# One level of Strassen's scheme for w_up, and w_down as a stage of its own, in a float32 two-block transformer step

## The chip, the cores and the metric

The kernel runs on one core of one Trainium2 chip. The metric is the device time of one execution in microseconds. PE is TensorE, DVE VectorE, ACT ScalarE, POOL GpSimd and SP SyncE, which issues the DMAs here.

## What is computed

Two transformer blocks on 1024 tokens of width 1024, in float32. The change lies in the last part of the second block, a feed-forward network with a short causal convolution over the tokens on one half of its hidden width, and the gate of a per-token embedding behind it. In outline, with h the normalized input:

```python
a, b = jnp.split(h @ w_up, 2, axis=-1)          # w_up: 1024 x 6144
hidden = gelu(conv3(a, ffn_conv_w, ffn_conv_b)) * b   # conv3: three taps, causal, per channel
x = x + rms_norm(hidden @ w_down, g_ffn_post)   # w_down: 3072 x 1024
gate = sigmoid(rms_norm(x, g_ple_gate) @ w_ple_gate)
out = x + gate * rms_norm(p @ w_ple_proj, g_ple_post)
```

## The kernel before, in words

**Precision.** Every float32 product is made of three matmuls of a rounded type (`mm3`, L229 to L235): both operands are split into a high part and the rest (`split`, L73 to L79: ACT rounds, DVE or POOL subtracts), and hi x hi, lo x hi and hi x lo are added up in one PSUM bank. A bank holds 128 x 512; there are eight, five of them under the name mm and three under tr.

**Weights.** A `Chunk` is a piece of a weight. `queue` puts chunks in a list, and `pump` fetches the next one as soon as a raw buffer is free (a DMA on SP, L183, tile wr) and splits it as soon as a pair of buffers wh and wl is free. The program is written with a clock of its own (`tick`, `later`), by which later steps of norm chains are put between the matmuls; the order on each engine comes from that and from a scheduler behind it, and on the chip each engine works through its own order.

**Up.** h is kept transposed in h3h and h3l (its high part and rest), k along partitions, 1024 tokens along the columns. The 3072 hidden channels come in 24 chunks of 128; each chunk c has two blocks of w_up (the one that is convolved, u, and the one that multiplies it). `dense_t_steps` takes a block and one half of the tokens (512 columns): eight k-tiles, 24 matmuls into one bank. The first four blocks take the first half of the tokens before the second, because the norm chains of the last tokens (`mix_add`, L2020: POOL adds to tile max, L2030 nxn, then transposes on PE, L328) still run. `ffn` (L2063) holds `emit`: for a u block ACT copies the bank to fu (L2080) and starts fg (L2081), DVE adds the two earlier taps (L2084, twice), ACT applies Gelu (L2087). For a b block DVE multiplies (L2090) and the result is split into fhh and fhl.

**Down.** `contract` takes two chunks of hidden, and for each of eight token tiles and two column halves it adds six matmuls in a bank and then, on DVE, the bank to the tile acc in SBUF (L2105). Eleven contracts lie between the up blocks, the last two behind them. Every tile of acc is complete only in the last one.

**Behind it.** `finish_pair` (L2275), for two token tiles at a time, is a chain of squares (ACT), rstd and norm (DVE, L2297), residual (POOL, L2298), squares, rstd and xn (DVE, L2306), and transposes (`to_hT`, L322). It feeds the product with w_ple_gate, 48 matmuls for each token tile (tiles fhT, flT), whose result og is multiplied and added (L2264, L2265) and stored.

Of the kernel before, what the change touches and what calls it, by code (L numbers as in the profile page):

```python
# [15 lines left out]
F32 = mybir.dt.float32  # L17
# [31 lines left out]
class Chunk:  # L49


    def __init__(self, pieces, shape):
        self.pieces, self.shape = pieces, shape
        self.raw = self.hl = self.pool = self.rpool = None
        self.half = 0


class Kernel:
# [127 lines left out]

    def split_w(self, c):
        for e in self.wpools:
            if e[2] < e[1] and (e[3] is None or id(c) in e[3]):
                e[2] += 1  # L190
                c.pool = e
                c.hl = [e[0].tile(c.shape, F32R, name=n, tag=n, bufs=e[1]) for n in ("wh", "wl")]
                self.lo_engs = self.lo_engs[1:] + self.lo_engs[:1]
                self.split(*c.hl, c.raw, self.lo_engs[0], self.hi_eng)
                c.raw = None
                c.rpool[2] -= 1
                return True
        return False

    def need(self, c):  # L200
        assert c.hl is not None, "weight buffers"
        return c.hl
# [1860 lines left out]
    def ffn(self, pools, pu, acc, up, down, before_last, last):  # L2063


        nc = self.nc
        NC, G = DFF // P, 2
        st = {}

        def emit(b, half, ps):  # L2070
            c, hs, o = b // 2, slice(half * 512, half * 512 + 512), half * 512
            if b % 2 == 0:
                if half == 0:
                    st[c] = (pu.tile([P, 2 + S], F32, name="fu", tag="fu", bufs=2),
                             pu.tile([P, S], F32, name="fg", tag="fg", bufs=2),
                             *(pools[c // G % 2 == 0].tile([P, S], F32R, name=n, tag=n, bufs=G)
                               for n in ("fhh", "fhl")))
                    nc.gpsimd.memset(st[c][0][:, :2], 0.0)  # L2078
                u, g = st[c][:2]
                nc.scalar.activation(u[:, 2 + o:2 + o + 512], ps, AF.Copy)  # L2080
                nc.scalar.activation(g[:, hs], ps, AF.Identity, scale=self.fc_w[:, 2 * NC + c:2 * NC + c + 1],  # L2081
                                     bias=self.fc_b[:, c:c + 1])
                for k in range(2):
                    nc.vector.scalar_tensor_tensor(g[:, hs], u[:, k + o:k + o + 512],  # L2084
                                                   self.fc_w[:, k * NC + c:k * NC + c + 1], g[:, hs],
                                                   op0=OP.mult, op1=OP.add)
                nc.scalar.activation(g[:, hs], g[:, hs], AF.Gelu_apprx_tanh)  # L2087
            else:
                _, g, hi, lo = st[c]
                nc.vector.tensor_tensor(g[:, hs], ps, g[:, hs], op=OP.mult)  # L2090
                self.split(hi[:, hs], lo[:, hs], g[:, hs])

        def contract(c0, tiles=range(NT)):
            ws = [self.need(down[c]) for c in range(c0, c0 + G)]
            for t in tiles:
                ts = slice(t * P, (t + 1) * P)
                for n in range(2):
                    cs = slice(n * 512, n * 512 + 512)
                    ps = self.mmt()
                    for i in range(G):  # L2100
                        hi, lo = st[c0 + i][2:]
                        self.mm3(ps, (hi[:, ts], lo[:, ts]), (ws[i][0][:, 0, cs], ws[i][1][:, 0, cs]),
                                 i == 0, i == G - 1)
                    if c0:
                        nc.vector.tensor_add(acc[:, t, cs], acc[:, t, cs], ps)  # L2105
                    else:
                        nc.scalar.activation(acc[:, t, cs], ps, AF.Copy)
                last(c0 + G == NC, t)
            if NT - 1 in tiles:
                for c in range(c0, c0 + G):  # L2110
                    self.free(down[c])
                    del st[c]

        for n, _ in enumerate(self.dense_t_steps(up, self.hT, emit, first=4)):
            c = (n + 1) // 4 - 1
            if (n + 1) % 4 == 0 and c % G == 0 and c >= G:
                contract(c - G, range(NT if c < NC - G else 4))
        before_last()
        for tiles in (range(4), range(4, NT)):
            if tiles[0]:  # L2120
                contract(NC - 2 * G, tiles)
            contract(NC - G, tiles)

    def block2(self, es):
# [66 lines left out]
        up, down = [], []  # L2191
        for c in range(DFF // P):
            up += [self.chunk_t(blk(wu, i * DFF + c * P), KT) for i in range(2)]
            down.append(Chunk([(lambda r: r[:, 0], wd[c * P:(c + 1) * P])], [P, 1, D]))
        with ExitStack() as es2:
            self.add_w(es2, "wow", 2, side="right", only=sum(ch_o, []))
            self.mix_add(self.pool(es2, "onp", side="right"), ch_o, mT, a["g_mix_post_2"][0], a["g_ffn_pre_2"][0], self.hT)
            for c in range(DFF // P):
                self.queue(up[2 * c:2 * c + 2])
                if c % 2 == 0 and c:  # L2200
                    self.queue(down[c - 2:c])
            self.queue(down[-2:])
            self.until(lambda: self.hcount == NT)
        es_m.close()

        acc = self.pool(es, "accp", side="right").tile([P, NT, D], F32, name="acc")
        es_f, es_u, es_x = (ExitStack() for _ in range(3))
        pools = [self.pool(es_f, n, side="right") for n in ("ffnp", "ffnq")]
        self.add_w(es_f, "ffx", 2, side="right", only=up[:-4] + down[:-2])
        self.add_w(es_u, "ffw", 1, 2, side="right", only=up + down[:-4])  # L2210
        ch_p, fin = [], {}

        def before_last():
            es_u.close()
            es_h.close()
            self.hcount = 0
            self.add_w(es_x, "plew", 4)
            fp = fin["pool"] = self.pool(es_x, "finp")
            fin["g"], fin["gp"], fin["ge"] = (self.row(fp, a[n][0], D, n[:8]) for n in
                                              ("g_ffn_post_2", "g_ple_gate_2", "g_ple_post_2"))  # L2220
            fin["r"] = fp.tile([P, NT], F32, name="pler")
            nc.vector.tensor_add(self.ple_ss[:, 0], self.ple_ss[:, 0], self.ple_ss[:, 1])
            self.rstd(fp, fin["r"], self.ple_ss[:, 0], D)
            ch_p.extend(self.chunks_n(a["w_ple_gate_2"][0][:, c * 512:c * 512 + 512], KT, 512) for c in range(2))

        def step(p, n):
            for _ in range(n):
                next(fin[p], None)

        def last(b, t):  # L2230
            if (b, t) == (1, 1):
                fin.update({p: self.finish_pair(fin, acc, 2 * p) for p in range(4)})
            for p, n in {(1, 1): [(0, 1)], (1, 3): [(0, 2), (1, 1)], (0, 5): [(0, 1)], (0, 7): [(1, 2), (0, 1)], (1, 5): [(1, 1)], (1, 7): [(1, 1)]}.get((b, t), ()) if fin else ():
                step(p, n)

        self.ffn(pools, self.pool(es_u, "ffnu", side="right"), acc, up, down, before_last, last)
        es_f.close()

        self.add_w(es_f, "plex", 2, side="right")
# [10 lines left out]
        with self.tc.manual_schedule(engines={mybir.EngineType.Activation}):  # L2250
            for t in range(2):
                emb(t)
            for t in range(NT):
                p = t // 2
                x, e = fin["x", t], embs.pop(0)
                for c in range(2):
                    cs = slice(c * 512, c * 512 + 512)
                    ps = self.mmt()
                    for k in range(KT):
                        wh, wl = self.need(ch_p[c][k // 2])  # L2260
# [161 lines left out]
```

## Time and profile before

| | |
|---|---|
| median of 3 runs | 3548.86 us (3547.29 to 3552.15) |
| the profiled execution | 3554.52 us, of it span 3552.8 us |
| mean granted TensorE clock | 0.957 |
| busy: PE, DVE, ACT, POOL | 3224.1, 2231.8, 1546.0, 946.5 us |
| feed-forward stage, first to last w_up matmul | 2592.1 to 3376 us |
| w_ple_gate | 3425 us to the end |

A busy share is an average over stages with different limits. The stage that is changed starts at 2592 us; what bounds it is read from its own stretches. A matmul's duration (some 395 ns) is its time through the pipeline; the distance from one to the next is what counts, and it is read from how many start in a stretch.

### The profile page before, as it was taken

The numbers are of one execution on the slowest core, as the hardware profiler recorded it, in microseconds if no ns is written. First come the engines' busy times: TensorE is split into PE (matmuls) and PEld (weight loads), VectorE is DVE, ScalarE is ACT, GpSimd is POOL, SyncE is SP. The second block draws the span as 40 slices with busy tenths as digits, with TensorE's granted clock in tenths as the row PEclk, the third lists the DMA queues.
The fourth block names the chain that finished last, engine by engine and source line by source line (L and its number), as shares of the span: only waits on it lengthen the run. The fifth ranks groups of instructions, "written<-read, shape, count | busy, mean of one in ns | idle before, by whom it ended". The sixth has DMA issues, their size and how long they took to land. (4 is left out here: it accounts for less than half of the span.)

```text
span 3552.8 us, 40896 instructions
## 1 busy us (share of the span) xinstructions
PE 3224.1 (91%) x14381; PEld 2577.9 (73%) x14381; DVE 2231.8 (63%) x3579; ACT 1546.0 (44%) x2354; POOL 946.5 (27%) x704
## 2 busy tenths in 40 slices
PE   7987799789898898998888999999989999999987
PEld 4865577567677677777666887888668888888866
DVE  6799954578656899999885644124563444444364
ACT  3553222578523666666565763211343222222232
POOL 2133223355104666666440220000110000000024
PEclk9998899799999899999899999999999999999998
DMA  5211376662545899999864214333431111111032
GB/s 191 66 46 56 121 225 190 149 175 62 163 156 188 311 319 318 315 326 323 275 204 150 69 60 147 101 119 98 143 119 48 48 48 48 48 48 48 18 130 83
DMA packets 351644, 510.66 MB, mean 144 GB/s; under 512 B 32140, under 2 KB 183072, under 8 KB 351436
## 3 DMA queue, kind: packets, MB, share of 16 engines
q1 hardware_dynamic: 330304, 465.78, 40.4%
q0 software_dynamic: 11440, 24.77, 2.6%
q10 hardware_dynamic: 9692, 17.48, 1.5%
q8 instruction: 114, 1.87, 0.2%
q14 instruction: 94, 0.77, 0.1%
HBM read 426.47 MB, written 76.20 MB: 141 GB/s over the span
## 5 line engine op out<-in xcount | busy, mean ns | idle before, releaser
L79 DVE TENSOR_TENSOR wl<-wr,wh 128x1024 fp32r<-128x1024 f32 (+1 forms) x441 | 752.5, 1729 | 428.7 <-ACT wh L76 427.9
L76 ACT ACTIVATE wh<-wr 128x1024 fp32r<-128x1024 f32 x564 | 587.5, 1053 | 749.8 <-PE mm L234 234.9
L79 POOL TENSOR_TENSOR wl<-wr,wh 128x1024 fp32r<-128x1024 f32 x145 | 386.0, 2704 | 91.9 <-ACT wh L76 85.9
L235 PE MATMUL mm<-h3h,wl 128*128 128x512 f32 x768 | 303.8, 396 | 5.5 <-DVE wl L79 3.1
L234 PE MATMUL mm<-h3l,wh 128*128 128x512 f32 x768 | 303.4, 395 | 0.2 <-DVE h3l L79 0.2
L233 PE MATMUL mm<-h3h,wh 128*128 128x512 f32 x768 | 303.5, 395 | 0.0
L233 PE MATMUL mm<-h2h,wh 128*128 128x512 f32 x576 | 229.5, 399 | 1.2 <-ACT h2h L76 1.2
L235 PE MATMUL mm<-h2h,wl 128*128 128x512 f32 x576 | 227.4, 395 | 0.0
L234 PE MATMUL mm<-h2l,wh 128*128 128x512 f32 x576 | 227.3, 395 | 0.0
L2078 POOL MEMSET fu<- 128x2 f32 x24 | 2.3, 100 | 687.4 <-DVE fg L2084 682.7
L233 PE MATMUL mm<-wh,hTh 128*128 128x512 f32 (+1 forms) x368 | 145.6, 396 | 40.2 <-POOL wh L78 17.6
L235 PEld LDWEIGHTS mm<-h3h,wl 128*128 128x128 f32 x768 | 144.5, 188 | 41.1 <-DVE wl L79 4.4
L2105 DVE TENSOR_TENSOR acc<-acc,mm 128x512 f32<-128x512 f32 x176 | 119.0, 685 | 87.8 <-PE mm L235 87.7
L233 PEld LDWEIGHTS mm<-h3h,wh 128*128 128x128 f32 x768 | 144.5, 188 | 34.6 <-ACT wh L76 0.5
L234 PEld LDWEIGHTS mm<-h3l,wh 128*128 128x128 f32 x768 | 144.5, 188 | 34.6 <-DVE h3l L79 0.5
L233 PE MATMUL mm<-wh,fhh 128*128 128x512 f32 x384 | 149.8, 393 | 5.8 <-ACT wh L76 3.1
L234 PE MATMUL pb<-wl,xgh 128*128 128x512 f32 x256 | 110.2, 430 | 48.6 <-DVE wl L79 47.4
L234 PE MATMUL mm<-wl,fhh 128*128 128x512 f32 x384 | 151.7, 395 | 0.0
L235 PE MATMUL mm<-wh,fhl 128*128 128x512 f32 x384 | 151.3, 394 | 0.0
L234 PE MATMUL mm<-wl,hTh 128*128 128x512 f32 (+1 forms) x368 | 142.2, 386 | 5.5 <-POOL wl L79 4.9
L235 PE MATMUL mm<-wh,hTl 128*128 128x512 f32 (+1 forms) x368 | 141.8, 385 | 0.0
L2020 POOL TENSOR_TENSOR max<-max,antmp 128x512 f32<-128x512 f32 x16 | 27.3, 1726 | 418.9 <-DVE antmp L2019 383.0
(615 smaller groups left out, 8063.9 us busy)
## 6 DMA issues: line engine op xcount, KB each, us to landing
wr<-in_exp_w SPq DMA_DIRECT2D x384, 512.0 KB
wr<-in_w_in SPq DMA_DIRECT2D x72, 512.0 KB
wr<-in_w_up SPq DMA_DIRECT2D x48, 512.0 KB
sg_d<-sg SPq DMA_DIRECT2D x64, 256.0 KB
score<-in_ada_w ACTq DMA_DIRECT2D x32, 512.0 KB
wr<-in_w_down SPq DMA_DIRECT2D x24, 512.0 KB
ar<-in_ada_w SPq DMA_DIRECT2D x16, 512.0 KB
x<-in_x SPq DMA_DIRECT2D x16, 512.0 KB
```

Of the source, the lines that this page charges most:

```text
L76: self.nc.scalar.activation(hi, x, AF.Copy)
L79: (lo_eng or self.nc.vector).tensor_tensor(lo, x, hi.bitcast(F32), op=OP.subtract)
L233: mm(ps, w[0], x[0], start=first, stop=False)
L234: mm(ps, w[0], x[1], start=False, stop=False)
L235: mm(ps, w[1], x[0], start=False, stop=last)
L2020: nc.gpsimd.tensor_tensor(x[:, cs], x[:, cs], tmp, op=OP.add)
L2078: nc.gpsimd.memset(st[c][0][:, :2], 0.0)
L2105: nc.vector.tensor_add(acc[:, t, cs], acc[:, t, cs], ps)
```

## The change

The first two chunks stay as they are. For the other 22, each product of a 128-channel pair of blocks with h is cut in quarters (the two blocks u and v; upper and lower half of k; first and second half of the tokens), and seven products of quarters, four k-tiles or 12 matmuls each, replace eight. Sums of weights (kinds s and d) and of operands (t1 to t4, which takes the place of one quarter of h) are made in float32 and then split; the results are put together from PSUM by DVE and, from SBUF, by POOL. hidden goes to DRAM (hid_d) in place of being split at once. When all of it is there, `ffn_down` multiplies it with w_down in two halves of the tokens, with all eight PSUM banks accumulating over the 24 chunks; w_down is loaded and split once for each half. The finishing chains of the first half's tokens are written into the second half, those of the others behind it.

```diff
+    def split_part(self, c, hi, lo):
+        u, v = (x.raw for x in c.pair[:2])
+        a, b = slice(0, 4), slice(4, 8)
+        f = self.sums.tile([P, KT, P], F32, name="wsum", tag="wsum", bufs=1) if c.kind in "sd" else None
+        def rest():
+            nc.scalar.activation(hi, f, AF.Copy)
+            nc.vector.tensor_tensor(lo, f, hi.bitcast(F32), op=OP.subtract)
+            c.ready = True
...
+        gp = lambda i, x, y, op: nc.gpsimd.tensor_tensor(f[:, i], x, y, op=op)
+        if c.kind == "u":
+            self.split(hi, lo, u)
+        elif c.kind == "v":
+            self.split(hi[:, a], lo[:, a], v[:, b])
+        elif c.kind == "s":
+            gp(a, v[:, a], v[:, b], OP.add)
+            gp(b, f[:, a], u[:, a], OP.subtract)
+            self.later(3.5, rest)
+        else:
+            gp(a, u[:, a], v[:, a], OP.subtract)
+            gp(b, u[:, b], v[:, b], OP.subtract)
+            gp(b, f[:, b], f[:, a], OP.add)
+            self.later(5.0, rest)
+    def fast_operands(self, pool, tmp):
...
+        for n, x2 in enumerate(x2s):
...
+            sub(gp, y, f(h12[1]), f(h11[1]))
+            sub(dv, x1, f(h12[0]), f(h11[0]))
+            yield 2.5
+            add(dv, x1, x1, y)
+            sub(gp, x3, f(h22[1]), f(h12[1]))
+            yield 2.5
+            self.split(*o1, x1)
+            sub(gp, y, f(h22[0]), f(h12[0]))
+            yield 2.5
+            sub(dv, x2, f(h22[0]), x1)
+            add(gp, x3, x3, y)
+            yield 2.5
+            add(gp, x2, x2, f(h22[1]))
+            self.split(*o3, x3)
+            yield 2.5
+            self.split(*o2, x2)
+            sub(gp, x2, f(h21[0]), x2)
+            add(gp, x2, x2, f(h21[1]))
...
-    def ffn(self, pools, pu, acc, up, down, before_last, last):
+    def ffn_up(self, pu, up, pairs, es_t):
...
+        for c, (u, s, d, v) in enumerate(pairs, len(up) // 2):
+            new(c)
+            g = st[c]
+            up0, up1 = (us[c % 2][:, 2 + n * 512:514 + n * 512] for n in range(2))
+            nc.scalar.activation(s1, product(u, 0, x["b11"]), AF.Copy)
+            add(nc.vector, up0, s1, product(u, 4, x["b21"]))
+            self.free(u)
+            gate(c, 0, up0)
+            nc.scalar.activation(s5, product(s, 0, x["t1"]), AF.Copy)
+            add(nc.vector, s2, s1, product(s, 4, x["t2"]))
+            self.free(s)
+            add(nc.vector, s3, s2, product(d, 0, x["t3"]))
+            add(nc.gpsimd, s2, s2, s5)
+            add(nc.gpsimd, s5, s3, s5)
+            add(nc.vector, up1, s2, product(d, 4, x["b22"]))
+            self.free(d)
+            gate(c, 1, up1)
+            add(nc.vector, s3, s3, product(v, 0, x["t4"]))
+            self.free(v)
+            nc.vector.tensor_tensor(g[:, half(0)], s3, g[:, half(0)], op=OP.mult)
+            nc.gpsimd.tensor_tensor(g[:, half(1)], s5, g[:, half(1)], op=OP.mult)
+            store(c)
+    def ffn_down(self, acc, hid, down, half, after):
+        ps = [self.trt() for _ in range(3)] + [self.mmt() for _ in range(5)]
+        for k in range(nk):
+            (xh, xl), (wh, wl) = self.need(hid[k // 2]), self.need(down[k])
+            for i in range(8):
+                ts, cs = slice(i // 2 * P, i // 2 * P + P), slice(i % 2 * 512, i % 2 * 512 + 512)
+                self.mm3(ps[i], (xh[:, k % 2, ts], xl[:, k % 2, ts]), (wh[:, 0, cs], wl[:, 0, cs]),
+                         k == 0, k == nk - 1)
+                if k == nk - 1:
+                    self.nc.scalar.activation(acc[:, 4 * half + i // 2, cs], ps[i], AF.Copy)
+                after(k, i)
...
-        self.ffn(pools, self.pool(es_u, "ffnu", side="right"), acc, up, down, before_last, last)
+        self.later_steps(0.0, self.fast_operands(fp, self.pool(es_t, "fastt")))
+        self.ffn_up(pu, up, pairs, es_t)
+        for half in range(2):
+            for k in range(0, NC, 2):
+                self.queue([hid[half][k // 2], *down[half][k:k + 2]])
...
+        self.ffn_down(acc, hid[0], down[0], 0, lambda k, i: None)
+        todo = {(0, 7): [0], (2, 7): [0], (4, 7): [0, 1], (6, 7): [0, 1], (8, 7): [1],
+                (NC - 1, 4): [0], (NC - 1, 6): [0]}
+        self.ffn_down(acc, hid[1], down[1], 1, lambda k, i: step(*todo.get((k, i), ())))
```

**First place: POOL at the start of the stage.** max is the residual of one token tile, to which POOL adds antmp in two halves; the last tile is the one named last. fty, ftx2 and ftx3 are the operand sums of `fast_operands`. Before:

```order
L2020 TENSOR_TENSOR max_21613<-max_21613,antmp_21628 128x512
L2020 TENSOR_TENSOR max_21613<-max_21613,antmp_21631 128x512
L2020 TENSOR_TENSOR max_21701<-max_21701,antmp_21716 128x512
L2020 TENSOR_TENSOR max_21701<-max_21701,antmp_21719 128x512
L2078 MEMSET fu_21835 128x2
```

And now:

```order
L2128 TENSOR_TENSOR max_21614<-max_21614,antmp_21629 128x512
L2128 TENSOR_TENSOR max_21614<-max_21614,antmp_21632 128x512
L272 TENSOR_TENSOR fty_21811<-h3l_20795 128x1024
L272 TENSOR_TENSOR ftx3_21813<-h3l_20795 128x1024
L238 TENSOR_TENSOR wsum_22023<-wsum_22023,wr_21788 128x512
L272 TENSOR_TENSOR fty_21811<-h3h_20794 128x1024
L273 TENSOR_TENSOR ftx3_21813<-ftx3_21813,fty_21811 128x1024
L273 TENSOR_TENSOR ftx20_21809<-ftx20_21809,h3l_20795 128x1024
L2128 TENSOR_TENSOR max_21702<-max_21702,antmp_21717 128x512
L2128 TENSOR_TENSOR max_21702<-max_21702,antmp_21720 128x512
```

Six operations for the Strassen operands and weights now stand between the adds of the last two token tiles.

**Second place: POOL in the steady state,** one pair with what lies on both sides of it. The first two rows make s of the next pair but one, fs2, fs5 and fg belong to a pair of products, and the two wsum rows between the fg rows make d (three operations).

```order
L238 TENSOR_TENSOR wsum_22688<-wr_22489 128x512
L238 TENSOR_TENSOR wsum_22688<-wsum_22688,wr_22487 128x512
L2228 TENSOR_TENSOR fs2_22551<-fs2_22551,fs5_22553 128x512
L2228 TENSOR_TENSOR fs5_22553<-fs3_22552,fs5_22553 128x512
L2249 TENSOR_TENSOR fg_22554<-fs5_22553,fg_22554 128x512
L238 TENSOR_TENSOR wsum_22731<-wr_22487,wr_22489 128x512 x2
L238 TENSOR_TENSOR wsum_22731<-wsum_22731 128x512
L238 TENSOR_TENSOR wsum_22831<-wr_22632 128x512
L238 TENSOR_TENSOR wsum_22831<-wsum_22831,wr_22630 128x512
L2228 TENSOR_TENSOR fs2_22694<-fs2_22694,fs5_22696 128x512
L2228 TENSOR_TENSOR fs5_22696<-fs3_22695,fs5_22696 128x512
L2249 TENSOR_TENSOR fg_22697<-fs5_22696,fg_22697 128x512
```

Here POOL had nothing but one MEMSET of fu for each chunk; now it has eight operations a pair, and the sums d and s for later pairs stand between fg of one pair and fs2 of the next.

**Third place: DVE in the same pair.** wl<-wsum are the rests of s and d, wl<-wr those of v (128x512) and u; L2228 are the sums with a bank, L2188 the taps of the convolution.

```order
L228 TENSOR_TENSOR wl_22687<-wsum_22688,wh_22686 128x1024
L2228 TENSOR_TENSOR fu0_21798<-fs1_22693,mm_22713 128x512
L228 TENSOR_TENSOR wl_22730<-wsum_22731,wh_22729 128x1024
L2188 SCALAR_TENSOR_TENSOR fg_22697<-fu0_21798,colsc_9279,fg_22697 128x512 x2
L2228 TENSOR_TENSOR fs2_22694<-fs1_22693,mm_22753 128x512
L89 TENSOR_TENSOR wl_22770<-wr_22489,wh_22769 128x512
L2228 TENSOR_TENSOR fs3_22695<-fs2_22694,mm_22777 128x512
L2228 TENSOR_TENSOR fu0_21798<-fs2_22694,mm_22793 128x512
L89 TENSOR_TENSOR wl_22808<-wr_22630,wh_22807 128x1024
L2188 SCALAR_TENSOR_TENSOR fg_22697<-fu0_21798,colsc_9279,fg_22697 128x512
L2228 TENSOR_TENSOR fs3_22695<-fs3_22695,mm_22815 128x512
L2188 SCALAR_TENSOR_TENSOR fg_22697<-fu0_21798,colsc_9279,fg_22697 128x512
```

The adds into acc are gone from here. The rest of s waits behind the last product of the pair before, and the second sum into fu0 (up1) waits for POOL's fs2.

## Rows read from the trace of the kernel before

**Rows 1.** Stretches of time: us, busy us and count by engine, clock, DMA.
```profile
core 0: us, PE busy (x) PEld busy (x) DVE busy (x) ACT busy (x) POOL busy (x), PEclk, DMA share, GB/s
...
2592.00:2640.00 48.00, 37.61 (x170) 28.27 (x170) 39.59 (x97) 22.11 (x37) 14.25 (x10) 1.00 0.46 144
...
2800.00:2900.00 100.00, 100.00 (x434) 81.30 (x433) 46.87 (x63) 20.79 (x28) 0.30 (x3) 1.00 0.14 43
...
3340.00:3380.00 40.00, 39.04 (x168) 31.08 (x167) 15.05 (x23) 7.59 (x11) 0.00 (x0) 1.00 0.00 1
...
3380.00:3425.00 45.00, 36.01 (x153) 27.79 (x151) 37.99 (x80) 17.51 (x24) 12.82 (x5) 0.96 0.52 175
...
3425.00:3553.00 128.00, 103.15 (x432) 82.36 (x432) 59.75 (x108) 37.07 (x58) 51.38 (x27) 0.89 0.26 87
...
3480.00:3490.00 10.00, 3.76 (x14) 3.25 (x15) 7.83 (x15) 2.61 (x4) 4.29 (x3) 0.57 0.32 108
```

**Rows 2.** Matmuls by tile: w_up (h3h), w_down (fhh), gate (fhT): ns min/median/max.
```profile
L233 PE MATMUL mm<-h3h,wh x768: 387/394/505, 2592.1 to 3376.0; 128*128 128x512 f32 x192
...
L233 PE MATMUL mm<-wh,fhh x384: 387/389/628, 2675.3 to 3423.1; 128*128 128x512 f32 x192
...
L233 PE MATMUL mm<-wh,fhT x128: 388/396/792, 3425.5 to 3546.5; 128*128 128x512 f32 x128
```

**Rows 3.** Groups of instructions in 2700 to 3300: count, busy us, mean ns, idle before.
```profile
L2105 DVE TENSOR_TENSOR acc<-acc,mm 128x512 f32<-128x512 f32 x144 | 98.1, 686 | 82.9 <-PE mm L235 82.9
...
L79 DVE TENSOR_TENSOR wl<-wr,wh 128x1024 fp32r<-128x1024 f32 x54 | 65.4, 1223 | 66.5 <-ACT wh L76 66.5
...
L76 ACT ACTIVATE wh<-wr 128x1024 fp32r<-128x1024 f32 x54 | 56.3, 1058 | 283.8 <-issue 180.3 <-PE mm L234 103.5
...
L2084 DVE SCALAR_TENSOR_TENSOR fg<-fu,colsc,fg 128x512 f32<-128x512 f32 x72 | 54.1, 752 | 76.6 <-ACT fg L2081 75.3
...
L2081 ACT ACTIVATE fg<-mm,colsc 128x512 f32<-128x512 f32 x36 | 27.8, 773 | 0.0
...
L79 DVE TENSOR_TENSOR fhl<-fg,fhh 128x512 fp32r<-128x512 f32 x36 | 24.8, 688 | 12.6 <-ACT fhh L76 12.6
...
L2087 ACT ACTIVATE fg<-fg 128x512 f32<-128x512 f32 x36 | 22.8, 632 | 59.0 <-DVE fg L2084 59.0
```

**Rows 4.** The same for POOL's L2020 (all; 2592 to 2642) and DVE's splits, 1400 to 1700.
```profile
L2020 POOL TENSOR_TENSOR max<-max,antmp x16: 1264/1294/2337, 2532.4 to 2621.7; 128x512 f32<-128x512 f32 x16
...
L2020 POOL TENSOR_TENSOR max<-max,antmp 128x512 f32<-128x512 f32 x8 | 14.1, 1787 | 47.5 <-ACT maj L2044 30.3 <-DVE antmp L2019 11.6 <-issue 5.6
...
L79 DVE TENSOR_TENSOR wl<-wr,wh 128x1024 fp32r<-128x1024 f32 x112 | 235.0, 2130 | 15.1 <-ACT wh L76 14.8
```

**Rows 5.** Timeline of the stage's start: start us, us, engine, line, instruction.
```profile
2601.85 3.52 POOL L2020 TENSOR_TENSOR max<-max,antmp 128x512 f32<-128x512 f32 x2 [5.61 <-issue]
...
2620.45 3.51 POOL L2020 TENSOR_TENSOR max<-max,antmp 128x512 f32<-128x512 f32 x2 [5.95 <-DVE antmp L2019]
...
2602.37 1.85 DVE L79 TENSOR_TENSOR wl<-wr,wh 128x1024 fp32r<-128x1024 f32 x1
...
2631.48 1.22 DVE L79 TENSOR_TENSOR wl<-wr,wh 128x1024 fp32r<-128x1024 f32 x1
...
2628.75 1.06 PE L328 MATMUL tr<-ident,nxn 128*128 128x128 f32 x8 [0.96 <-DVE nxn L2030]
```

**Rows 6.** PE's waits from 3425 (us, times, longest), groups from 3380, last matmul.
```profile
PE tr L328 <- DVE fxn L2306: 17.7, 3, 8.8
...
L2298 POOL TENSOR_TENSOR acc<-acc,fx 128x1024 f32<-128x1024 f32 x8 | 23.8, 3001 | 23.3 <-DVE acc L2297 21.2 <-PE mm L235 2.1
...
L2306 DVE SCALAR_TENSOR_TENSOR fxn<-acc,fr,g_ple_ga 128x1024 f32<-128x1024 f32 x8 | 9.9, 1279 | 0.3
...
3547.01 0.39 PE L235 MATMUL mm<-wh,flT 128*128 128x512 f32 x1
```

**Rows 7.** Transfers to and from x_d, from issue to landing.
```profile
DMA to landing us min/median/max: 3.2/8.9/10.7
```

More of the change, by code (lines that the diff above doesn't have):

```diff
@@ L2061, in mix_add @@
             self.dense_n(ch, src, lambda t, ps: emit(t, i % 2, ps), range(4 * (i // 2), 4 * (i // 2) + 4))
-    def ffn(self, pools, pu, acc, up, down, before_last, last):
+    def ffn_up(self, pu, up, pairs, es_t):
         nc = self.nc
-        NC, G = DFF // P, 2
+        NC = DFF // P
+        us = [pu.tile([P, 2 + S], F32, name=f"fu{i}") for i in range(2)]
+        for u in us:
+            nc.gpsimd.memset(u[:, :2], 0.0)
         st = {}
-        def emit(b, half, ps):
-            c, hs, o = b // 2, slice(half * 512, half * 512 + 512), half * 512
-            if b % 2 == 0:
[L2073 to L2087, printed above, removed]
-            else:
[L2089 to L2122, printed above, removed]
@@ new lines, in ffn_up, with product @@
+        for _ in self.dense_t_steps(up, self.hT, emit, first=4):
+            pass
+        self.until(lambda: not self.chains)
+        self.fast_last()
+        es_t.close()
+        x = self.fast
+        def product(chunk, o, m):
+            ps = self.mmt()
+            wh, wl = self.need(chunk)
+            for k in range(4):
+                self.mm3(ps, (wh[:, o + k], wl[:, o + k]), (m[0][:, k], m[1][:, k]), k == 0, k == 3)
+            return ps
+        for c, (u, s, d, v) in enumerate(pairs, len(up) // 2):
+            add = lambda e, out, p, q: e.tensor_tensor(out, p, q, op=OP.add)
+            s1, s2, s3, s5 = (pu.tile([P, 512], F32, name=n, tag=n) for n in ("fs1", "fs2", "fs3", "fs5"))
+            new(c)
+            g = st[c]
[17 more added lines that the diff above has]
+            nc.gpsimd.tensor_tensor(g[:, half(1)], s5, g[:, half(1)], op=OP.mult)
+            store(c)
@@ L2190, in block2 @@
         wu, wd = a["w_up_2"][0], a["w_down_2"][0]
[L2191 to L2194, printed above, removed]
+        NC, plain = DFF // P, 2
+        self.hid_d = self.dram.tile([NC, P, S], F32, name="hid_d")
+        blocks = [[blk(wu, i * DFF + c * P) for i in range(2)] for c in range(NC)]
+        up = [self.chunk_t(b, KT) for x in blocks[:plain] for b in x]
+        pairs = [self.fast_parts(*x) for x in blocks[plain:]]
+        hid, down = [], []
+        for half in range(2):
+            hid.append([Chunk([(lambda r: r, self.hid_d[k:k + 2, :, half * 512:half * 512 + 512]
+                                .rearrange("k p c -> p k c"))], [P, 2, 512]) for k in range(0, NC, 2)])
+            down.append([Chunk([(lambda r: r[:, 0], wd[k * P:(k + 1) * P])], [P, 1, D]) for k in range(NC)])
         with ExitStack() as es2:
@@ L2197, in block2 @@
             self.mix_add(self.pool(es2, "onp", side="right"), ch_o, mT, a["g_mix_post_2"][0], a["g_ffn_pre_2"][0], self.hT)
[L2198 to L2202, printed above, removed]
+            self.queue(up)
+            for x in pairs:
+                self.queue(x)
             self.until(lambda: self.hcount == NT)
         es_m.close()
-        acc = self.pool(es, "accp", side="right").tile([P, NT, D], F32, name="acc")
@@ new lines, in block2, with step @@
+        fin["r"] = fp.tile([P, NT], F32, name="pler")
+        nc.vector.tensor_add(self.ple_ss[:, 0], self.ple_ss[:, 0], self.ple_ss[:, 1])
+        self.rstd(fp, fin["r"], self.ple_ss[:, 0], D)
+        fin.update({p: self.finish_pair(fin, acc, 2 * p) for p in range(4)})
+        def step(*pairs):
+            for p in pairs:
+                next(fin[p], None)
+        self.ffn_down(acc, hid[0], down[0], 0, lambda k, i: None)
+        self.add_w(es_x, "plew", 4, only=ch_p)
+        self.queue(ch_p)
```

131 lines of the change are left out of this document (99 added, 32 removed).

## The prediction

> **What bounds the kernel now.** I read the stretches by time first, then the groups of instructions of the up and down stage, then the timeline at the stage's start, and the waits of TensorE last. In the stretches [rows 1] the reader is to see that PE is busy for the whole of every steady stretch of the feed-forward stage (100.00 of 100 us at full granted clock), while DVE stands at 47, ACT at 21 and POOL at 0.30 of 100 us. So between 2640 and 3340 us only the number of matmuls counts: 434 in 100 us, or 0.2306 us each (100 / 434 = 0.2304; over ten stretches it comes to 0.2306). The counts [rows 2] are 768 x 3 = 2304 matmuls for w_up, 384 x 3 = 1152 for w_down and 128 x 3 = 384 for the gate behind them. The ends of the stage are another matter: 10.4 us of PE are idle in 2592 to 2640, and from 3340 on PE waits, and its granted clock is 0.96, then 0.89 on average [rows 1]. In one 10 us stretch of these, behind the longest wait of PE (8.8 us [rows 6]), it is 0.57: nearly all at the lower of the two levels, 1.2 GHz, where 1.00 is 2.4 GHz.
>
> **The change part by part.** The profiled execution took 3554.5 us (span 3552.8); the median of the runs shown is 3548.9, 5.7 less. I sum against 3554.5 and take the 5.7 off at the end.
>
> *Matmuls removed.* 22 of the 24 pairs of blocks take seven products of 12 matmuls (84) where they took eight (96): 22 x 12 = 264 fewer, and the order of PE shows 264 rows fewer in all. Every one stood in a stretch where PE never waited, so 264 x 0.2306 = **-60.9 us**. The Trainium skill (TensorE: Matmul & The Clock Gate, Back-to-back issue gap) gives N/2.4 + 2.5 = 216 ns for 512 columns; by it the term would be 57.0. The trace has 230.6 ns, and that is used.
>
> *The tail.* Before, the norm chains of the output (finish_pair) start only when the last contract is done, because every tile of acc needs all 24 chunks. PE waits 17.7 us in three waits for fxn behind 3425 us [rows 6]. Now half the tokens are finished 133 us earlier (576 matmuls x 0.2306), so the chains of pairs 0 and 1 lie beside matmuls, and those of pairs 2 and 3 have 22 to 44 us of gate matmuls between the steps. A chain is about 21 us: eight passes over 128x1024 (squares, norms, xn) of at most 1.28, two POOL adds of 3.0 [rows 6], and two short rstd. So the waits go. What goes, from [rows 1]: 1.0 + 9.0 + 24.9 us idle in the last three stretches, less the 5.4 from the last matmul to the end [rows 6], which stays; and what the lower clock cost, 103.2 - (384 x 0.2306 + 48 transposes x 0.133 = 95.0) = 8.2 and 36.0 - (137 x 0.2306 + 16 x 0.133 = 33.7) = 2.3. The transpose's 0.133 is 1.06 / 8 [rows 5]. Sum 40; I leave 1 for the first tile's transposes: **-39 us** (bounds -25 and -40).
>
> *The start.* On POOL five adds of 128x1024 and one of 128x512 (t1 to t4) now stand ahead of the two adds for the last token tile (first place of the order). At twice 1.294 and at 1.294 [rows 4] that is 14.2 us; POOL idled 5.95 there [rows 5]. The last tile's transposes, on which PE waited at 2628.75 [rows 5], come 8 us later; some of this overlaps a wait PE has anyway. **+7 us** (3 to 12). The first Strassen pair needs d, whose sums stand behind nine more such adds: 9 x 2.6 + 3 x 1.3 + split = 30 us after the last tile, and PE gets there after 144 matmuls, 33 us. Cover just holds: **+2 us** (0 to 4).
>
> *One pair in the steady state, the term that decides.* PE needs 84 x 0.2306 = 19.4 us. Added work by group [rows 3, 4]: POOL 8 x 1.294 = 10.4; DVE 3.5 splits x 1.223 + five sums with PSUM x 0.686 + four gate steps x 0.752 + one product of that size 0.69 = 11.4; ACT 3.5 x 1.058 + 2 x 0.773 + 2 x 0.632 and two copies of at most 0.773 = under 8.1. No engine's sum is over 19.4. But the orders (second and third place) make a loop: POOL's fg of pair c, then d of c+2 (3 adds), ACT's rounding of d, DVE's rest of d, then POOL's s (it reuses the single wsum buffer, 2 adds), fs2, then DVE's sum for up1, a split, a gate step, the sum of the seventh product, a gate step, ACT's Gelu, and POOL's fg of c+1.
>
> What the two engines do to each other is in the timeline [rows 5]: the split of 2602.37 takes 1.85 us beside two POOL adds that take 3.52 together; alone they are 1.22 and 2 x 1.29. 1.22 + 2.58 = 3.80, so the three went nearly one after the other. Over the expert stage the same split means 2.130 [rows 4]. So I let operations of DVE with two SBUF inputs and POOL's alternate, and count those that fall between: 7 POOL adds x 1.294 = 9.06; ACT 1.058 + 0.632 = 1.69; DVE three splits 3.67, the half split of v 0.69, four gate steps 3.01, two sums 1.37, and 0.6 for a split that waits for fs5. Sum **20.1 us**, 0.7 over PE: 22 x 0.7 = **+15 us**. Lower bound: without the alternation both gate steps of the first half, the split of v and the 0.6 leave the loop, 17.3 us, PE bounds and the term is 0. Upper bound: under the second and third rival. I take 20.1 because the timeline's stretch has the very same pair of operations. The Trainium skill (SBUF — State Buffer, SBUF: two separate sides) calls the port pair that the two engines share "an exclusive lock, not a bandwidth split"; the 1.85 us agree. By that rule the loop is 20.1, without it PE's 19.4.
>
> *The turn to w_down.* SP holds the rows of the norms until the last w_up product, and the last store of hid until POOL's fg, some 3.7 us after it; behind them stand the w_down chunks for k = 2 and 3. A load lands in 3.2 to 10.7 us [rows 7], a split takes 2.3, the deadline is 48 matmuls or 11.1 us: between in time and 5.6 late, and once more for the next. **+5 us** (0 to 11).
>
> *At nothing.* The DVE adds into acc go (0.686 each [rows 3]) and the reload of hid comes, with one more pass over w_down: per two k 1.5 MB and three splits, 3.7 us of DVE and 3.2 of ACT, beside 11.1 us of matmuls. The 24 stores of hid lie beside 19 us of matmuls each. If that cover went, 72 loads and splits would show where 24 stood.
>
> Sum: 3554.5 - 60.9 - 39 + 7 + 2 + 5 + 15 = 3483.6; less 5.7, **3478 us**.
>
> **Rivals.** *PE stays the bound* in the pairs: the alternation costs less than I count, since some waits fall where the chain waits for PE anyway. For it: no engine over 60% by its own sum. 3468.6 - 5.7 = **3463**. *A longer loop:* POOL's adds mean 1.787 in the stretch where DVE splits beside them [rows 4]; if half of the 3.5 us more per pair fall on the loop it is 21.8: 22 x 2.4 = 53 and **3516**. Against it: there the splits that caused it are already counted by me. *Slower than before:* the loop at fully contended prices, seven adds at 1.787 and three splits at 2.130, is 20.1 + 3.5 + 2.7 = 26.3 us, 22 x 6.9 = 152 and **3615**. This decides from 19.4 + (3549 - 3463) / 22 = 23.3 us per pair. Against it: the one wait would be counted on both engines. *The change does not remove the matmuls* (plain blocks, or more of them elsewhere): the order of PE excludes it.
>
> **Chances.** Forecast 0.42, PE-bound 0.35, longer loop 0.17, the fully contended loop 0.06 (of it 0.02 near no change). 0.2% is 7 us, about what a measurement tells from no change. Faster 0.94, same 0.02, slower 0.04. Range: from PE-bound with the start at 3, the first pair and the turn at 0 (3452) to a little over the longer loop (3521).
>
> **What would show it.** In the changed profile: PE matmuls 264 fewer; Strassen pairs at 19.4 us if PE-bound, 20.1 if the loop binds, then with PE waiting for PSUM sums by DVE; splits beside POOL over 1.3 us; the wait of PE on the last tile's transposes some 7 us longer; w_down stretches at 434 matmuls in 100 us; no wait for fxn and granted clock near 1.00 behind w_down. It would be wrong if a pair took over 22 us, if w_down waited for its loads throughout, or if the tail kept its waits.

## The result and the profile after

The changed kernel takes **3526.8 us** (median; 3521.2 to 3530.1) against 3550.5 for the kernel before: a ratio of 0.9928, interval [0.9906, 0.9951]. It is faster, by 24 us where 71 were forecast, and 6 us above the range. The profiled execution has a span of 3528.4 us.

First the matmuls by tile (count, shortest/median/longest in ns, first and last start), the answer to [rows 2]. m2h is the w_o stage ahead of the change; fhh in the kernel before and `mm<-wl,wh` in the changed one are w_down, the latter five of its eight PSUM banks, which end last. The first two rows are the kernel before.

```profile
L233 PE MATMUL mm<-wh,m2h x128: 387/394/628, 2486.7 to 2591.3; 128*128 128x512 f32 x128
...
L234 PE MATMUL mm<-wl,fhh x384: 388/394/775, 2675.6 to 3423.4; 128*128 128x512 f32 x192
```
```profile
L341 PE MATMUL mm<-wh,m2h x128: 387/394/775, 2490.4 to 2594.4; 128*128 128x512 f32 x128
...
L341 PE MATMUL mm<-h3h,wh x416: 387/394/795, 2595.2 to 3120.7; 128*128 128x512 f32 x139
...
L342 PE MATMUL mm<-wl,wh x240: 387/389/628, 3123.7 to 3398.6; 128*128 128x512 f32 x120
...
L341 PE MATMUL mm<-wh,fhT x128: 389/394/797, 3399.2 to 3522.2; 128*128 128x512 f32 x128
```

They cut the span in three. Up to the last w_o matmul: 2591.3 before, 2594.4 now, +3.1, and nothing in there was changed (over the profiles of this study this point lies between 2582 and 2594). From there to the last matmul of w_down: 832.1 before (to 3423.4), 804.2 now (to 3398.6), **-27.9**. From there to the end: 129.4 before, 129.8 now, **+0.4**. The forecast had -44.2 for the second (-60.9 + 7 + 2 + 15 + 5, and 12.3 of the tail's term, which lie ahead of 3425: 10.0 of idle time and 2.3 of clock) and -26.7 for the third. So 16 of the 49 us missing were lost in the stage and 27 in the tail; 3 are the first part, and the rest is that this profiled execution lies 3.3 above its median and not 5.7. The stage as a whole, before and then now:

```profile
2591.30:3423.40 832.10, 812.77 (x3507) 654.61 (x3506) 386.51 (x582) 226.88 (x324) 27.89 (x36) 1.00 0.19 58
```
```profile
2594.40:3398.60 804.20, 762.84 (x3241) 609.36 (x3240) 476.12 (x573) 291.76 (x383) 334.02 (x206) 0.98 0.34 110
```

PE is busy for 49.9 us less and idle for 22.0 us more (19.3 before, 41.4 now). The stretches of the changed kernel (columns as in [rows 1]):

```profile
2592.00:2640.00 48.00, 28.21 (x125) 21.07 (x123) 43.31 (x93) 17.11 (x29) 28.17 (x16) 0.91 0.43 129
2640.00:2700.00 60.00, 45.61 (x174) 35.38 (x173) 52.58 (x41) 20.95 (x28) 39.91 (x18) 0.87 0.14 47
...
2800.00:2900.00 100.00, 99.99 (x425) 78.94 (x424) 60.69 (x70) 36.21 (x50) 60.08 (x42) 1.00 0.25 79
...
3100.00:3200.00 100.00, 95.34 (x401) 76.76 (x400) 48.65 (x56) 34.53 (x39) 13.90 (x8) 0.97 0.52 177
3200.00:3300.00 100.00, 97.56 (x422) 79.73 (x421) 50.62 (x79) 38.99 (x50) 12.32 (x4) 0.99 0.45 151
...
3340.00:3380.00 40.00, 40.00 (x177) 32.88 (x176) 15.48 (x13) 13.23 (x13) 0.00 (x0) 1.00 0.48 157
...
3425.00:3460.00 35.00, 25.81 (x112) 20.78 (x112) 15.70 (x36) 11.01 (x18) 11.28 (x7) 0.90 0.21 67
3460.00:3500.00 40.00, 28.03 (x118) 22.42 (x118) 14.70 (x26) 11.43 (x18) 16.93 (x10) 0.81 0.21 73
```

The reader is to see three places. In the steady pairs PE never shows an idle moment, with POOL at 60 and DVE at 61 of 100 us. At the start PE now stands idle for 19.8 + 14.4 = 34.2 us where it was 10.4, and the granted clock is 0.91 and 0.87, partly the lower level. Behind 3425, where the forecast had no waits, it stands for 9.2 + 12.0 us at a clock of 0.90 and 0.81. The waits of PE, in 2592 to 2720 and then in 3380 to 3530 (the answer to [rows 6]; us in total, times, longest), name who ends them:

```profile
PE tr L436 <- DVE anr L411: 12.6, 2, 10.7
PE mm L341 <- DVE fg L2209: 8.1, 1, 8.1
PE tr L436 <- DVE nxn L2138: 5.4, 2, 3.8
```
```profile
PE mm L341 <- ACT fhT L86: 23.3, 3, 10.5
```

**The start.** The timeline of DVE there (start, us, instruction), then that of POOL:

```profile
2626.21 0.14 DVE L403 TENSOR_SCALAR nr<-nr 128x1 int32<-128x1 int32 x1
...
2628.81 2.21 DVE L411 SCALAR_TENSOR_TENSOR nr<-rst,nr 128x1 f32<-128x1 f32 x1
...
2632.26 2.10 DVE L411 SCALAR_TENSOR_TENSOR anr<-rst,anr 128x1 f32<-128x1 f32 x1
...
2665.25 3.42 DVE L272 TENSOR_TENSOR ftx<-h3h,ftx 128x1024 f32<-128x1024 f32 x1
2668.59 3.42 DVE L89 TENSOR_TENSOR ft1l<-ftx,ft1h 128x1024 fp32r<-128x1024 f32 x1
```
```profile
2628.66 2.34 POOL L272 TENSOR_TENSOR fty<-h3h 128x1024 f32<-128x1024 f32 x1 [1.22 <-DVE ftx L273]
2631.08 3.27 POOL L273 TENSOR_TENSOR ftx<-ftx,fty 128x1024 f32<-128x1024 f32 x1
...
2639.64 2.53 POOL L2128 TENSOR_TENSOR max<-max,antmp 128x512 f32<-128x512 f32 x2 [2.99 <-DVE antmp L2127]
...
2664.21 3.38 POOL L272 TENSOR_TENSOR fty<-h3h 128x1024 f32<-128x1024 f32 x1
2667.67 3.27 POOL L273 TENSOR_TENSOR ftx<-ftx,fty 128x1024 f32<-128x1024 f32 x1
```

A step of rstd on a single column (128x1) takes 2.21 us on DVE and ends with the POOL sum that began at 2628.66, and the one of 2632.26 ends with the sum of 2631.08; from 2655 to 2672, the sums and splits of DVE take 3.2 to 3.4 us, as long as the POOL sums beside them. POOL then waits 2.99 us for DVE's antmp ahead of the last tile's max adds: POOL's queue, which the forecast counted, was not what was late, DVE's was.

**The tail.** ScalarE's timeline behind 3425:

```profile
3428.72 1.15 ACT L2399 ACTIVATE ple<-ple,pler 128x1024 f32<-128x1024 f32 x1 [6.53 <-DMA ple<-ple_d]
3429.77 1.55 ACT L86 ACTIVATE fhT<-tr 128x512 fp32r<-128x512 f32 x3
```

There are three such places (3429, 3465 and 3497). Each of PE's three waits ends with fhT, and each fhT stands in ScalarE's queue right behind a scaling of ple (emb) that waits for its load. The two buffers of ple come free only when a token tile is through, so the load is issued at the moment when its data are wanted.

### The profile page after: what moved, and what is told of

It is laid out like the page before. It is cut to its first block, busy times and chain, and to the rows that moved or that the text cites. A ratio compares the mean times of both kernels' runs of the same rounds, so it can differ in the third digit from the quotient of the medians.

```text
span 3528.4 us, 40979 instructions
## 1 busy us (share of the span) xinstructions
PE 3170.0 (90%) x14117; PEld 2531.6 (72%) x14117; DVE 2314.9 (66%) x3549; ACT 1604.9 (45%) x2406; POOL 1247.4 (35%) x872
## 5 line engine op out<-in xcount | busy, mean ns | idle before, releaser
L86 ACT ACTIVATE wh<-wr 128x1024 fp32r<-128x1024 f32 (+1 forms) x612 | 624.6, 1037 | 579.2 <-PE mm L342 179.5
L341 PE MATMUL mm<-wh,hTh 128*128 128x512 f32 (+1 forms) x368 | 145.1, 394 | 39.0 <-POOL wh L88 17.6
L343 PE MATMUL mm<-h3h,wl 128*128 128x512 f32 x416 | 165.2, 398 | 4.4 <-DVE ans L401 2.4
L341 PE MATMUL mm<-h3h,wh 128*128 128x512 f32 x416 | 167.4, 403 | 1.5 <-ACT wh L86 1.2
L342 PE MATMUL mm<-h3l,wh 128*128 128x512 f32 x416 | 165.2, 397 | 0.0
L341 PEld LDWEIGHTS mm<-h2h,wh 128*128 128x128 f32 x576 | 108.5, 188 | 27.5 <-ACT h2h L86 1.5
L342 PEld LDWEIGHTS mm<-h2l,wh 128*128 128x128 f32 x576 | 108.5, 188 | 26.2 <-issue 1.2
L343 PEld LDWEIGHTS mm<-h2h,wl 128*128 128x128 f32 x576 | 108.4, 188 | 25.2
L341 PE MATMUL mm<-hTh,wh 128*128 128x512 f32 x256 | 106.4, 416 | 19.6 <-POOL wh L88 12.1
L1409 DVE TENSOR_TENSOR ptl<-tr,pth 128x512 fp32r<-128x512 f32 x192 | 102.5, 550 | 26.0 <-ACT pth L1408 24.7
L342 PE MATMUL pa<-wl,xgh 128*128 128x512 f32 x256 | 103.4, 404 | 17.0 <-DVE wl L89 14.0
```

Of the source, the lines that this page charges most:

```text
L86: self.nc.scalar.activation(hi, x, AF.Copy)
L341: mm(ps, w[0], x[0], start=first, stop=False)
L342: mm(ps, w[0], x[1], start=False, stop=False)
L343: mm(ps, w[1], x[0], start=False, stop=last)
L1409: self.lag.append(lambda c0=c0, th=th, tl=tl, tr=tr: nc.vector.tensor_tensor(tl[:, c0:], tr[:, c0:], th[:, c0:].bitcast(F32), op=OP.subtract))
```

## The experiments

The runs were made in several sets, each beside the kernel before, whose median lay between 3547.6 and 3550.5 in them; a difference of two medians from different sets is good to some 3 us.

**The tail's load alone.** `emb` is split: the load one token tile ahead, with a third buffer.

```diff
+            def load(t): ... pl.tile(..., tag="ple", bufs=3); dma_start(...)
             for t in range(NT):
+                load(t + 2)
                 x, e = fin["x", t], embs.pop(0)
```


> Edit: in the tail the load of the embedding rows (ple) is issued one token ahead of its scaling, into a third buffer; nothing else moves. Theory A (ScalarE's in-order queue stands on that load, and the fhT halves that PE wants are queued behind it): PE's three waits for fhT, 23.3 us together in the changed kernel, go, and with them most of what the clock lost there; 20 to 28 us faster than the changed kernel (3527), so near 3502. Theory B (the chain of norms, squares and sums of a pair is itself too long for the matmuls beside it): the waits stay under the name of another producer and the time falls by under 5 us.

Measured: 3494.3 us, 0.9842 [0.9818, 0.9865], 32 under the changed kernel. PE's waits from 3300 on:

```profile
PE mm L341 <- ACT fhT L86: 2.8, 3, 0.9
PE tr L436 <- DVE flT L89: 1.6, 1, 1.6
```

The same three waits fell from 23.3 to 2.8 us, the last part of the span from 129.8 to 105.4 (3395.1 to 3500.5): -24.4, as theory A has it. The granted clock in 3460 to 3500 is 0.98, from 0.81. What the medians have beyond that is not in the part that was edited (its profile reaches the last w_o matmul 4.6 us earlier). The edit moves the load and adds a buffer at once; which of the two is needed was not tried.

**The operand sums on DVE.**

```diff
-        dv, gp = nc.vector, nc.gpsimd
+        dv, gp = nc.vector, nc.vector
```


> Edit: the 18 operand sums of 128x1024 that stood on POOL run on DVE. Theory A (POOL's wide adds and DVE's operations shut each other out, so that a 1.21 us sum on DVE costs less than a 2.36 us one on POOL, and the rstd steps of the last norm tiles no longer stand behind POOL): the DVE operations of 3.35 to 3.43 us in 2622 to 2695 fall to 1.2, PE's idle time in 2592 to 2720 falls from 34 us to 14 to 26, 8 to 20 us faster than the changed kernel: 3507 to 3519. Theory B (the sums are too much work ahead of the last tile wherever they stand; DVE's queue takes POOL's place): within 5 us of 3527, or slower by up to 10.

Measured: 3507.5 us, 0.9884 [0.986, 0.9908], 19 under the changed kernel. From the last w_o matmul (2582.1) to the last of w_up it takes 509 us against 526. PE's waits in 2580 to 2720 come to 17.6 us, of which one is large, and DVE's sums take their 1.22 us:

```profile
PE tr L436 <- DVE nxn L2138: 10.7, 2, 10.4
```
```profile
2609.85 1.22 DVE L272 TENSOR_TENSOR ftx<-h3h 128x1024 f32<-128x1024 f32 x1
```

Theory A, with a miscount in the expectation: POOL had 14 of these sums and DVE 6, not 18 and 6. DVE does 20 sums where it did 6, and PE's idle time at the start is 17.6 us where it was 34.2. Giving the sums to the idle engine was what cost that time. The wait of 10.4 that stays is of theory B's kind, the sums ahead of the last norm tile in DVE's queue; it is tried further down.

**Both edits.**

> Edit: the edits of the early ple load and of the sums on DVE together. If both theories A hold, the gains add, as they lie 700 us apart: 28 to 48 us under the changed kernel, 3479 to 3499. If only the tail's holds, near 3502.

Measured: 3479.2 us, 0.9807 [0.9782, 0.9831]: the gains add (48 us). The time is that of the forecast to 1 us, and this is in part luck: it is another kernel than the forecast's, in which DVE does the sums, and errors of single terms cancel. PE's waits at the start are 18.8 us against 10.4 (+8.4, forecast +7 and +2), the turn and the middle of w_down 7.0 (forecast 5), the last part 105.4 (-24.0, forecast -26.7), and a pair costs less than the forecast's 20.1.

**No Strassen**, the stage of w_down and the tail kept.

```diff
-        NC, plain = DFF // P, 2
+        NC, plain = DFF // P, 24
-        self.later_steps(0.0, self.fast_operands(...))
```


> Edit: all 24 chunks of w_up as plain blocks (768 x 3 matmuls again), no operand sums; w_down as a stage from DRAM, its loads and the new finishing order stay. Theory A (the matmuls did go at 60.9 us, the start took 27 of it and the pairs 5 to 10 more, and the stage of w_down with its tail is worth nothing): 3550 to 3562. Theory B (the forecast's terms: the tail gave 39 and the turn cost 5): near 3516, that is 34 faster than the kernel before.

Measured: 3540.4 us, 0.9977 [0.9967, 0.9987], between the two, so neither theory has it. By its profile the stage (last w_o matmul 2590.5 to last of w_down 3412.6) is 822.1 us, 10.0 under the kernel before: w_down as a stage did remove most of the idle time ahead of 3425. Its tail is 133.0, 3.6 over: the ple waits again (24.1 us in three). So the matmuls, 60.9 us of work by the forecast, bring 13.6 of the 24 us (17.9 in the stage, by the two profiles); the start, the pairs and the turn take the rest. Its steady stretch is w_up alone, which gives the distance from one w_up matmul to the next, 400 / 1720 = 0.2326 us:

```profile
2700.00:3100.00 400.00, 400.00 (x1720) 322.98 (x1719) 119.92 (x142) 103.64 (x144) 0.00 (x0) 1.00 0.23 72
```

**Three more POOL adds in each pair.**

```diff
             gp(b, f[:, a], u[:, a], OP.subtract)
+            gp(b, f[:, a], u[:, a], OP.subtract)
         ...
             gp(a, u[:, a], v[:, a], OP.subtract)
+            gp(a, u[:, a], v[:, a], OP.subtract)
             gp(b, u[:, b], v[:, b], OP.subtract)
+            gp(b, u[:, b], v[:, b], OP.subtract)
```


> Edit to the changed kernel: three of POOL's five 128x512 adds for the weight sums of a pair run twice (two for d, one for s), 3 x 1.29 = 3.9 us more of POOL on the chain of every pair; the results are the same. Theory A (PE bounds a pair, and the chain through POOL, DVE and ScalarE has the 1.5 us of room that POOL's wait for DVE ahead of fs2 shows): a pair takes 19.8 + 3.9 - 1.5 = 22.2 us, 22 x 2.4 = 53 us more, near 3580. Theory B (the chain of the forecast, 20.1 us, already sets the pair): all of it shows, 22 x 3.9 = 86, near 3613. Theory C (POOL is busy for 60 of 100 us only, so there is room): within 10 us of 3527.

Measured: 3591.3 us, 1.0122 [1.0105, 1.0139], 64 over the changed kernel. POOL's timeline, of the changed kernel and then of this one, gives the pair from one fg to the next:

```profile
2875.00 2.10 POOL L2249 TENSOR_TENSOR fg<-fs,fg 128x512 f32<-128x512 f32 x1 [3.81 <-issue]
2877.06 2.57 POOL L238 TENSOR_TENSOR wsum<-wr 128x512 f32<-128x512 f32 x2
...
2883.43 1.75 POOL L238 TENSOR_TENSOR wsum<-wr 128x512 f32<-128x512 f32 x1 [2.43 <-DVE wl L228]
2885.26 1.62 POOL L238 TENSOR_TENSOR wsum<-wsum,wr 128x512 f32<-128x512 f32 x1
2888.38 2.66 POOL L2228 TENSOR_TENSOR fs<-fs,fs 128x512 f32<-128x512 f32 x2 [1.50 <-DVE fs L2228]
2894.84 2.09 POOL L2249 TENSOR_TENSOR fg<-fs,fg 128x512 f32<-128x512 f32 x1 [3.81 <-issue]
```
```profile
2878.13 2.09 POOL L2252 TENSOR_TENSOR fg<-fs,fg 128x512 f32<-128x512 f32 x1 [3.81 <-issue]
2880.18 5.04 POOL L238 TENSOR_TENSOR wsum<-wr 128x512 f32<-128x512 f32 x4
...
2890.84 3.54 POOL L238 TENSOR_TENSOR wsum<-wsum,wr 128x512 f32<-128x512 f32 x2
2894.34 2.67 POOL L2231 TENSOR_TENSOR fs<-fs,fs 128x512 f32<-128x512 f32 x2
2900.81 2.09 POOL L2252 TENSOR_TENSOR fg<-fs,fg 128x512 f32<-128x512 f32 x1 [3.80 <-issue]
```

The pair is 19.84 us in the changed kernel and 22.7 here. Both views show POOL's steps of the forecast's loop; in the changed kernel one of them waits for PE's side: the 1.50 ahead of fs2, for DVE's sum with d's first product. Here that wait is gone, and PE waits instead, which it does nowhere in the changed kernel's pairs (2800 to 3000 of this run):

```profile
PE mm L344 <- ACT fs L2240: 18.7, 8, 2.7
```

The three adds took 2.47 us in d (5.04 against 2.57) and 1.92 in s (3.54 against 1.62), 4.4 and not 3.9, as the one in s runs beside DVE. So 22.7 less 4.4 is a loop of **18.3 us**, and 19.84 less the wait of 1.50 gives the same; with 4.4 in theory A's sum the pair is 22.7 and the time 3590. PE bounds the pairs (A), with 1.5 us of room.

**The weight sums on DVE too** (from here on the kernel with both edits is the base).

```diff
-        gp = lambda i, x, y, op: nc.gpsimd.tensor_tensor(f[:, i], x, y, op=op)
+        gp = lambda i, x, y, op: nc.vector.tensor_tensor(f[:, i], x, y, op=op)
```


> Edit to the kernel of early ple load and operand sums on DVE (3479): the five weight sums of a pair also go from POOL to DVE, which takes 6.5 us of POOL out of the chain and puts 3.4 to 3.5 us of DVE in. Theory A (PE bounds the pair; matmuls 0.233 us apart are all there is): a pair stays at 19.6 to 19.85 us and the time within 5 us of 3479. Theory B (the chain sets the pair by a hair, and the 0.46 us over 19.37 are its waits): a pair at 19.4, 22 x 0.4 = 9 us faster, 3470.

Measured: 3470.1 us, 0.9782 [0.9766, 0.9799], 9 under its base (7.5 by the profiles, from the last w_o matmul on; the two intervals overlap a little). DVE's timeline repeats after 19.55 us:

```profile
2896.40 2.27 DVE L238 TENSOR_TENSOR wsum<-wr 128x512 f32<-128x512 f32 x2
...
2915.95 2.27 DVE L238 TENSOR_TENSOR wsum<-wr 128x512 f32<-128x512 f32 x2
```

and 2900 to 3000 has 431 matmuls, where the changed kernel has 425. So theory B in part. In 2800 to 3000 of the changed kernel no matmul waits, but PE's weight loads do, for sums of DVE and copies of ScalarE:

```profile
PEld mm L341 <- DVE fs L2228: 4.2, 10, 0.4
PEld mm L341 <- ACT fs L2237: 1.3, 7, 0.2
```

This run has none of them. They come to 0.55 us a pair, of which 0.29 shows in its length. What is left is the matmuls' own distance: 84 x 0.2326, from the run without Strassen, is 19.54.

**The last norm tiles ahead of the sums.** The sums take the second half of each block first; three or four plain chunks.

```diff
-        for n, x2 in enumerate(x2s):
+        for n, x2 in ((1, x2s[1]), (0, x2s[0])):
-        NC, plain = DFF // P, 2
+        NC, plain = DFF // P, 3        (4 in the second run)
```


> Edit to the kernel of 3479: the operand sums take the second half of each block first, whose data the last norm tiles write, so that no sum stands ahead of those tiles on DVE; and three chunks of w_up stay plain instead of two (12 matmuls more, 2.8 us, and 19 us more of cover). Theory A (PE's 9.8 us wait on the last tile's transposes is the sums ahead of it on DVE): that wait falls under 2 us; the sums end some 10 us later, under the longer cover; 3 to 8 us faster than 3479. Theory B (what is left at the start is the norm chain itself): the wait stays at 7 to 10, and the 2.8 us are added: 3480 to 3485.

> Edit as in the run with three plain chunks, with four. Theory A: the same wait goes, and no wait for the operand sums is left; the further 12 matmuls cost 2.8 us: within 3 us of the run with three plain chunks if those sums were covered there, and faster than it by up to 8 if they were not. Theory B: 2.8 us slower than the run with three.

Measured: 3481.3 us, 0.981 [0.9791, 0.9829], and 3483.2 us, 0.9817 [0.98, 0.9833]. The wait did go; PE's largest waits in 2580 to 2720 with three chunks:

```profile
PE mm L343 <- DVE wl L89: 4.5, 3, 2.4
...
PE tr L436 <- DVE anr L411: 1.9, 1, 1.9
PE tr L436 <- DVE nxn L2138: 1.3, 1, 1.3
```

So the cause is as theory A has it, but the time did not fall by it: the intervals of the three runs overlap. Counted from the last w_o matmul the profiles give 892.0 (base), 888.8 and 895.4 us. Whether the 3 us are real isn't settled by this. Part of the gain came back elsewhere: PE's waits at the turn and in the middle of w_down are 7.0 us in the base, 10.3 with three plain chunks and 14.8 with four, and each chunk adds 2.8 us of matmuls.

**The residual sums on DVE**, and with them the three plain chunks, on the kernel of 3470.

```diff
-            nc.gpsimd.tensor_tensor(acc[:, t], acc[:, t], xt[j], op=OP.add)
+            nc.vector.tensor_tensor(acc[:, t], acc[:, t], xt[j], op=OP.add)
```


> Edit to the kernel of 3470: only the residual sums of the finished pairs on DVE. Theory A (a split behind POOL's residual sum holds PE up for 2.4 us in the middle of w_down): that wait goes, 2 to 3 us faster, 3467 to 3468. Theory B (hidden otherwise): within 1 us of 3470.

> Edit to the kernel of 3470 (early ple load; operand and weight sums on DVE): three plain chunks with the operand sums behind the last norm tiles, and the two residual sums of each finished pair (128x1024) on DVE instead of POOL. If the gains add, the start gives 3 (as by the profiles of the run with three plain chunks: 892 against 889 us from the last w_o matmul on) and the 2.4 us wait on a split at the middle of w_down, beside POOL's residual sums, goes: 3464 to 3468. If DVE's own queue is full at the start (96 of 100 us were not free there), nothing or a loss: 3470 to 3476.

Measured: 3464.2 us, 0.9761 [0.9746, 0.9776], and **3461.3 us**, 0.975 [0.9733, 0.9767], the fastest of the study: 87 under the kernel before, 65 under the change. The 2.4 us wait on a split (wl) in the middle of w_down is in neither profile. The first is 6 us under its base, where its theory A had 2 to 3; by the profiles, from the last w_o matmul on, the three kernels take 884.5, 879.5 and 874.7 us. The two intervals overlap, so the share of the third plain chunk stays open.

**The early load in the kernel before.**

> Edit to the kernel before, nothing of the change in it: the ple load one token ahead in a third buffer. The forecast took PE's waits for fxn in its tail (17.7 us) to be the norm chains alone. Theory A (the same ple load stands in ScalarE's queue ahead of the squares and of fhT there too, with 7.5 to 8.4 us of ScalarE idle in front of each scaling): 8 to 25 us faster than 3548. Theory B (the norm chains bound that tail, as the forecast had it): under 5 us.

Measured: 3553.8 us, 1.0014 [1.0004, 1.0024]: no gain, theory B. Its waits from 3360 on name the norm chains as before:

```profile
PE tr L328 <- DVE fxn L2315: 25.7, 4, 13.5
```

The forecast had read that tail rightly. In the kernel before the late load was hidden behind the norm chains; the change took those away and the load came to light.

## Why the prediction was wrong

- **Matmuls removed, -60.9: right.** 2040 matmuls of w_up against 2304, and without Strassen the time is 13.6 higher, which is what is left of them when all that Strassen's other work takes is paid. The price of 0.2306 us is a little low: the count of a stretch takes in the one or two matmuls that straddle its edges, and w_down's lie closer than w_up's. At 0.2326 the term is -61.4, and the 84 matmuls of a pair take 19.54 us and not 19.37.
- **The tail, -39: the step that failed most.** Its part ahead of 3425 came in the main (12.3 forecast; the stage without Strassen is 10.0 shorter). Behind it, "So the waits go" was true of the waits for fxn and false of PE: -26.7 forecast, +0.4 measured, with PE waiting 23.3 us for fhT behind the ple load. By the forecast's own signs this alone made it wrong: the tail kept its waits. What is late next was not asked there. ScalarE's timeline of the kernel before shows the load, where it cost nothing yet:

```profile
3487.34 1.15 ACT L2246 ACTIVATE ple<-ple,pler 128x1024 f32<-128x1024 f32 x1 [8.25 <-DMA ple<-ple_d]
3488.40 1.55 ACT L76 ACTIVATE fhT<-tr 128x512 fp32r<-128x512 f32 x3
```

  With the load moved, the part is 105.4 long, 24.0 under the kernel before; the 2.7 to the forecast's 26.7 lie within PE's short waits there (2.8 and 1.6), where the forecast had kept 1 for the first tile's transposes. So the load was nearly all that this part of the term lacked.
- **The start, +7 and +2: mis-sized.** PE's idle time grew by 23.8 us (34.2 less 10.4), and the clock fell to 0.91 and 0.87: the 252 matmuls and 32 transposes of 2594.4 to 2700 took 71.4 us where 62.9 is their time at 0.2326 and 0.133. In the kernel before 139 and 32 took 38.3 against 36.6 (2591.3 to 2640), so the clock is worth some 7 us, an estimate. The forecast counted six POOL adds ahead of POOL's max adds. The rows show what stood in their place: 14 wide adds of 2.3 to 3.4 us, beside which DVE's sums, splits and single-column steps stood still, and the norm tiles are DVE's work. The forecast had this alternation, from [rows 5], and used it for the pairs alone.
- **The pair, +15: wrong in kind.** By the forecast's own 19.37 the term is 22 x (19.84 - 19.37) = 10.3, which looks near, but 22 x 0.17 of it is the distance of the matmuls; 22 x (19.84 - 19.54) = 6.6 is what the pair's waits cost, on PE's weight loads. The loop is there, but it is 18.3 us long and not 20.1, and PE bounds. The rival with PE as the bound (0.35) described this term; the longer loops did not come.
- **The turn, +5: right.** PE waited 4.1 us on a w_down split and 0.5 on the last sum. Another 2.4 in the middle of w_down, a split beside POOL's residual sums, was not forecast.
- **The sum of the stage**: matmuls -61.4, idle time and clock ahead of the last w_down matmul -8.9 and -2.3, start +23.8 and some +7 for the clock, pairs +6.6, turn and middle of w_down +7.0: -28.2, where -27.9 was measured.

The Trainium skill (SBUF — State Buffer, SBUF: two separate sides) says that whichever of the two engines starts first holds the shared pair for the whole instruction, and for DVE it names operations in a 2-port perf mode and, against a GpSimd operation that reads SBUF, those with two SBUF inputs. The start agrees as to the last: the single-column step with two SBUF tensors took 2.21 us, the one with one tensor 0.14 us at 2626.21, both beside a sum on POOL. Had the forecast costed the start by it, each of DVE's blocked steps there would have carried one POOL sum.

## What to carry to other kernels

When a change removes the wait that ends last, read the queue of every engine in that stage for the wait that lay under it, above all an in-order queue in which a transfer issued late stands ahead of what PE wants. Work given to an idle POOL is not free where DVE is on the path: here DVE did the same sums sooner alone than the two together. The margin of a loop is measured by lengthening it, with what was added taken from the new trace and not from the old price, and an engine that shows 100% busy may still hold waits of a few tenths of a microsecond.

## What was not expected of the hardware

- A small operation loses as much as a large one: 128x1 steps of 0.16 us took 1.9 to 2.2 beside POOL's 128x1024 sums, and sums of 1.22 took 3.4. The sums of DVE that read one operand from PSUM kept their 0.68 us throughout the pairs.
- POOL's 128x1024 sum takes 2.33 to 2.38 us where DVE leaves it alone, DVE's 1.22: the idle engine is half as fast as the one that it blocks.
- Full-clock matmuls of the same shape are not equally far apart: w_down in the changed kernel has 373 in 85 us (3305 to 3390, 0.228 us each as counted), plain w_up without Strassen 1720 in 400 (0.2326), the pairs with all weight sums on DVE 1248 in 290 (0.232), the steady stretch of the kernel before, which mixes w_up and w_down, 3020 in 700 (0.2318). The distance goes with the product and not with the kernel; the cause was not tried.
